# First feed-forward of a decoder block: seven block products for eight in four units of its last product, with a weight ring of five

## The chip, the cores and the metric

The kernel runs on one core of a Trainium2 chip. The time is the device time of one execution in microseconds (us), the median of several runs; shorter is better. The program is one launch, and all data start and end in the chip's main memory (HBM).

The engines are named as in the profile: PE is the matrix engine (PEld its weight loads), DVE the vector engine, ACT the scalar engine, POOL the general one, SP the engine that issues nearly all DMAs here. A matmul leaves its result in a PSUM bank of 128 x 512 float32, of which there are eight.

## The reference

One layer on 256 tokens of 1024 features, all in float32: a feed-forward, a token-mixing part, a second feed-forward, a last norm. What matters here is the first line:

```python
def swiglu(x, w_gate, w_up, w_down):
    return (jax.nn.silu(x @ w_gate) * (x @ w_up)) @ w_down

h = h + 0.5 * swiglu(rmsnorm(h, ffn1_norm), ffn1_w_gate, ffn1_w_up, ffn1_w_down)
n = rmsnorm(h, mix_norm)
z = n @ w_in                      # queries, keys, values and the gated branch, from n
# attention and spatial gating, sigmoid gates, one output projection, added to h
h = h + 0.5 * swiglu(rmsnorm(h, ffn2_norm), ffn2_w_gate, ffn2_w_up, ffn2_w_down)
return rmsnorm(h, final_norm)
```

The hidden width is 2816, so that `w_down` is 2816 x 1024: 22 blocks of 128 rows.

## The kernel before

**Three matmuls for a product.** Every float32 operand is split into a high part (a cast to the matrix engine's rounded float32, on ACT, L239) and a low part (value minus high part, on DVE, L241). A block product, 128 tokens x 128 features times 128 x 512 weights, is then three matmuls (`mm3`, L232 to L236): high by high, high by low, low by high.

**Weights come in units.** A unit is 1 MB in HBM, as a rule four 128 x 512 blocks, fetched as two halves of 512 KB into a ring of seven raw tiles (`RAW`, L161) and split into one tile of a ring of four (`RING`, pool `wp`). `unit(i, ahead)` (L200) sees to it that the splits of all units up to i + ahead stand in the programs of ACT and DVE before the matmuls of unit i; with `ALONE` that is three units ahead. A split of unit i + 3 or later overwrites a ring tile and so waits until PE has read its last occupant. Each split of a half also puts the fetch of the half seven places on into SP's queue, which waits until that raw tile is free.

**Order of work.** PE and SP do what they are told in the order of the program text. DVE and ACT are ordered by a scheduler in the two feed-forwards' first products, and by the text inside `with in_order():`, which holds the whole of the first feed-forward's last product and what follows it up to the second feed-forward. Each engine runs its own list strictly in order, and an instruction that waits holds up all behind it.

**First feed-forward.** Its first product runs in eleven chunks of 256 hidden features, two units each (`chunk`, L447; tiles `f`). Behind a chunk, `glu` (L486) makes the hidden values by tokens, and they go through HBM to be turned: `leave` writes a chunk (`f1way`), `arrive` reads four blocks of 128 hidden features back (`f1back`, one buffer), `settle` splits them (`f1h`). The last product (L658 to L677, tiles `down`) has 11 units f1d of four blocks each. It goes through the 1024 output features in two halves of 512: first half f = 0, all 22 hidden blocks for both token blocks j, then f = 1. At the end of a half, `add` (L640) adds the bank to the residual by tokens (`ht1`), transposes it in 32 x 32 squares, writes it to HBM (`h_way`) and squares it; `from_way` reads it back by features into `h`. `norm_parts(f)` (L653) makes high and low parts of the normed half (`nT2`) out of `h`. `norm_parts(0)` stands behind the ninth unit's matmuls. Then come q, k and gv: the products over the first half of the features for all three (`chunk(..., [0])`), `norm_parts(1)` among them, then those over the second half.

**Seven products for eight.** The second feed-forward's last product (`down`, L355) already treats the units in `SEVEN` = 0, 2, 4, 6 otherwise. A unit is there two hidden blocks by two feature halves, and with two token blocks a 2 x 2 by 2 x 2 block product of eight 128 x 128 x 512 products. Winograd's form of Strassen's scheme needs seven. It takes sums of the weight quarters (`quarters`, L175: four adds on DVE) and of the hidden blocks (`form`, L512: four DVE operations and a split). Such a unit fills two ring tiles: "single" (three quarters as they are) and "sums" (four sums); only the first is fetched. Products go to four banks of their own (`shared` 1, 5, 6, 7) and to the ordinary ones (`acc`). `settle_seven` (L402) folds the shared banks into the output with a copy on ACT, four adds and four multiply-adds on DVE.

## Time and profile before

| | us |
|---|---|
| median of 3 runs (lowest, highest) | 522.43 (522.08, 522.85) |
| the profiled execution's own time | 522.75 |
| its span, first to last instruction | 520.6 |
| PE busy in the span | 512.6 |
| DVE busy | 378.7 |
| ACT busy | 273.3 |
| mean of DMA traffic | 244 GB/s |

An execution's time is some 2 us longer than its span: 522.75 beside 520.6 here. The mean granted clock of the matrix engine is 0.998 of full speed. Durations in the rows are those of single instructions; neighbours on one engine overlap somewhat, so that the distance between two starts can be shorter than a duration. That is so above all for matmuls: one has a duration of 0.39 us and the next starts 0.23 us after it.

For orientation, the profile has the first product of the first feed-forward up to 125.6 us, its last product from there to 185.5 us, q, k and gv to 218 us, and the second feed-forward's last product from 456.9 to 511.7 us.

### The profile page before, as it was taken

To read this page: it belongs to the slowest core of one execution; us is meant where nothing else is said; L and a number is where in the kernel's file an instruction comes from. 1 tells how busy PE (TensorE), PEld (TensorE's weight loads), DVE (VectorE), ACT (ScalarE), POOL (GpSimd) and SP (SyncE) were. 2 spreads that over 40 slices of the span, in tenths; PEclk is the share of its full clock that TensorE was granted. 3 is DMA by queue.
4 is the path that set the end of the run, shared out by engine and by line. 5 is a ranking of instruction groups with operands and counts; after the bars stand their busy time and mean duration, and the time that the engine had idled before them with its cause. 6 is when DMAs were issued, how large, how long until landed. Compare 5 with 4: busy or idle time off the path is not lost.

```text
span 520.6 us, 6736 instructions
## 1 busy us (share of the span) xinstructions
PE 512.6 (98%) x2389; PEld 426.9 (82%) x2389; DVE 378.7 (73%) x533; ACT 273.3 (52%) x382; POOL 12.0 (2%) x25
## 2 busy tenths in 40 slices
PE   9999999999999999999999999999999999999995
PEld 7888888888888888888888898888888888888884
DVE  6895757576455565669977687987866776799974
ACT  7755355464444545666656423666535544566712
POOL 0010000000000010000000000001000000000002
PEclk9999999999999999999999999999999999999999
DMA  8998598969876867597799756839689869459602
GB/s 314 369 346 300 154 360 259 259 211 293 240 248 199 285 192 255 153 304 270 187 346 326 264 172 170 313 95 339 210 220 314 274 262 326 148 178 280 225 0 81
DMA packets 63920, 126.80 MB, mean 244 GB/s; under 512 B 11664, under 2 KB 36752, under 8 KB 63760
## 3 DMA queue, kind: packets, MB, share of 16 engines
q1 hardware_dynamic: 63600, 126.06, 75.3%
q8 instruction: 18, 0.29, 0.2%
q10 hardware_dynamic: 288, 0.33, 0.2%
q14 instruction: 14, 0.11, 0.1%
HBM read 113.26 MB, written 13.11 MB: 243 GB/s over the span
## 4 chain that ended last, share of the span: by engine, by line
PE 93%; DMA 3%; DVE 1%; ACT 1%; SPq 1%; issue 1%; POOLq 0%; DVEq 0%; POOL 0%; ACTq 0%
PE f L234 15%; PE f L236 15%; PE f L235 15%; PE down L236 4%; PE down L234 4%; PE down L235 4%; PE acch L235 4%; PE acch L236 3%; PE acch L234 3%; PE acc L208 3%; PE g L234 3%; PE g L236 3%; PE g L235 3%; PE acc L213 1%; DMA raw<-in_gate 1%; PE f L586 1%
## 5 line engine op out<-in xcount | busy, mean ns | idle before, releaser
L241 DVE TENSOR_TENSOR w<-raw,w 128x1024 fp32r<-128x1024 f32 (+1 forms) x180 | 209.5, 1205 | 62.7 <-ACT w L239 62.7
L239 ACT CAST w<-raw 128x1024 fp32r<-128x1024 f32 (+1 forms) x180 | 177.6, 1038 | 84.0 <-PE f L236 46.6
L234 PE MATMUL f<-w,n 128*128 128x512 f32 x336 | 130.9, 389 | 0.0
L236 PE MATMUL f<-w,n 128*128 128x512 f32 x336 | 130.9, 389 | 0.0
L235 PE MATMUL f<-w,n 128*128 128x512 f32 x336 | 130.8, 389 | 0.0
L236 PEld LDWEIGHTS f<-w,n 128*128 128x128 f32 x336 | 63.1, 188 | 13.1
L235 PEld LDWEIGHTS f<-w,n 128*128 128x128 f32 x336 | 63.1, 188 | 13.1
L234 PEld LDWEIGHTS f<-w,n 128*128 128x128 f32 x336 | 63.1, 188 | 12.9
L235 PE MATMUL down<-w,f1h 128*128 128x512 f32 x88 | 34.3, 390 | 0.0
L234 PE MATMUL down<-w,f1h 128*128 128x512 f32 x88 | 34.3, 389 | 0.0
L236 PE MATMUL down<-w,f1h 128*128 128x512 f32 x88 | 34.3, 389 | 0.0
L236 PE MATMUL acch<-w,f2h 128*128 128x512 f32 x64 | 24.9, 390 | 0.0
L235 PE MATMUL acch<-w,f2h 128*128 128x512 f32 x64 | 24.9, 390 | 0.0
L234 PE MATMUL acch<-w,f2h 128*128 128x512 f32 x64 | 24.9, 390 | 0.0
L234 PE MATMUL g<-w,n 128*128 128x512 f32 x64 | 24.9, 390 | 0.0
L235 PE MATMUL g<-w,n 128*128 128x512 f32 x64 | 24.9, 389 | 0.0
L236 PE MATMUL g<-w,n 128*128 128x512 f32 x64 | 24.9, 389 | 0.0
L490 ACT ACTIVATE f2s<-f,rstd 128x256 f32<-128x256 f32 x22 | 10.3, 473 | 24.5 <-PE f L236 24.3
L490 ACT ACTIVATE f1s<-f,rstd 128x256 f32<-128x256 f32 x22 | 10.3, 473 | 24.3 <-PE f L236 22.8
L492 DVE SCALAR_TENSOR_TENSOR f2a<-f,rstd,f2s 128x256 f32<-128x256 f32 x22 | 10.1, 472 | 14.7 <-ACT f2s L490 14.4
L235 PEld LDWEIGHTS down<-w,f1h 128*128 128x128 f32 x88 | 16.5, 188 | 3.4
L234 PEld LDWEIGHTS down<-w,f1h 128*128 128x128 f32 x88 | 16.5, 188 | 3.4
(207 smaller groups left out, 711.5 us busy)
## 6 DMA issues: line engine op xcount, KB each, us to landing
raw<-in_f SPq DMA_DIRECT2D x84, 512.0 KB, 6.2
raw<-in_f1d SPq DMA_DIRECT2D x22, 512.0 KB, 5.5
raw<-in_f2d SPq DMA_DIRECT2D x22, 512.0 KB, 6.4
raw<-in_gate SPq DMA_DIRECT2D x16, 512.0 KB, 6.3
raw<-in_out SPq DMA_DIRECT2D x8, 512.0 KB, 5.8
f1way<-f1t SPq DMA_DIRECT2D x11, 256.0 KB, 6.6
f2way<-f2t SPq DMA_DIRECT2D x11, 256.0 KB, 5.1
front<-in_first SPq DMA_DIRECT2D x7, 384.0 KB, 6.0
```

What stands on the lines that cost most here:

```text
L208: nc.tensor.matmul(ps, st, both.rearrange("p two n -> p (two n)"), start=first, stop=last)
L213: nc.tensor.matmul(ps[:, n:], st, both[:, 0, :], start=False, stop=False)
L234: nc.tensor.matmul(ps, sh, mh, start=first, stop=False)
L235: nc.tensor.matmul(ps, sh, ml, start=False, stop=False)
L236: nc.tensor.matmul(ps, sl, mh, start=False, stop=last)
L239: nc.scalar.copy(hi, src)
L241: nc.vector.tensor_sub(lo, src, hi.bitcast(F32))
L490: nc.scalar.activation(sg, ps[j][:, :CH], AF.Silu, scale=rs[j])
L492: nc.vector.scalar_tensor_tensor(a, ps[j][:, CH:], rs[j], sg, op0=ALU.mult, op1=ALU.mult)
L586: nc.tensor.matmul(sums[0][j][:, c], st[j][0], hi[:, c], start=k + c.start == 0, stop=False)
```

## The change

The first feed-forward's last product uses the seven-product form too, in the units of hidden blocks 0 and 1, 4 and 5, 8 and 9, 12 and 13. These four units (f1s, laid out as in the second feed-forward) have both feature halves in them. The other 14 hidden blocks (`REST`) stay in seven plain units (f1d) that go through the feature halves one after the other as before. The order is seven-unit, plain unit, four times, then three more plain units: eleven in all. The bytes fetched are the same.

- `settle_seven` is in two parts: first the adds into features 0 to 511, and, as a function that is called later, those into features 512 to 1023. The second feed-forward calls both at once. In the first, the first part stands behind the fourth seven-unit's matmuls, and the second behind the end of half f = 0, in the middle of the fourth plain unit. For that unit and the fourth seven-unit the look-ahead is 1, so that no later unit's split stands between those steps on DVE and ACT. `norm_parts(0)` stands behind the fifth plain unit, with two plain units left.
- `form_behind` makes the hidden blocks' sums during the first product, in both feed-forwards.
- `RING` is 5. `ALONE` and `PAIRED` keep their values of 3 and 2; the new `DEEP` is 4 and is used in both feed-forwards' products (from the fourth chunk of the first one, from the third of the second) and in both last products.
- The four sums of a "sums" unit are all made ahead of its two splits; before, two of them stood ahead of each split. They take the raw tiles out of use earlier.
- To make room, `h` and the two tiles of forms share memory one after the other, the zeros of the warm-up use the memory of a later tile, the banks' sums use the pool of the weights' sums, and the memory set aside for descriptors of DMAs that software issues is set to 1024 bytes.

```diff
-RING = 4
+RING = 5
 RAW = 7
-ALONE = RING - 1
-PAIRED = RING - 2
+DEEP = RING - 1
+ALONE = RING - 2
+PAIRED = RING - 3
 SEVEN = (0, 2, 4, 6)
+REST = [k for k in range(FB) if k // 2 not in SEVEN]
+PLAIN = len(REST) // 2
...
-    zeros = small.tile([P, S], BF16, tag="zeros", name="zeros", bufs=1)
+    zeros = act.tile([P, S], BF16, tag="ws", name="zeros")
...
-    f1d = add_units("f1d", FB // 2)
+    f1d = []
+    for n in range(PLAIN):
+        if n < len(SEVEN):
+            f1d.append((len(units), n))
+            units.extend([("f1s", n, "single"), ("f1s", n, "sums")])
+        f1d.append((len(units), None))
+        units.append(("f1d", n))
...
-            (a, b), (c, d) = ([raws[i - 1, k][:, 0, n:n + 512] for n in (0, 512)] for k in range(2))
-            r, to = sump.tile([P, 2, 512], F32, tag="sum", name=f"sum{i}_{hf}"), w[:, 2 * hf:2 * hf + 2]
             if hf == 0:
-                raws[i] = r
-                nc.vector.tensor_add(r[:, 0], a, b)
-                nc.vector.tensor_add(r[:, 1], b, d)
-            else:
-                nc.vector.tensor_add(r[:, 0], raws.pop(i)[:, 0], d)
-                nc.vector.tensor_add(r[:, 1], r[:, 0], c)
+                (a, b), (c, d) = ([r[:, 0, n:n + 512] for n in (0, 512)] for r in [raws.pop((i - 1, k)) for k in range(2)])
                 for k in range(2):
-                    del raws[i - 1, k]
+                    raws[i, k] = sump.tile([P, 2, 512], F32, tag="sum", name=f"sum{i}_{k}")
+                first, second = raws[i, 0], raws[i, 1]
+                nc.vector.tensor_add(first[:, 0], a, b)
+                nc.vector.tensor_add(first[:, 1], b, d)
+                nc.vector.tensor_add(second[:, 0], first[:, 0], d)
+                nc.vector.tensor_add(second[:, 1], second[:, 0], c)
+            r, to = raws.pop((i, hf)), w[:, 2 * hf:2 * hf + 2]
         return split(to[:, :, 0, :], to[:, :, 1, :], r)
...
+    def product(banks, name, key, st, w, last):
+        first = key not in banks
+        if first:
+            banks[key] = bank(f"acc{name}" + "_".join(map(str, key)))
+        mm3(banks[key], st, w, first, last)
+    def seven(name, at, i, tokens_of, acc, shared, ahead=DEEP):
+        a, b, d = tokens_of(2 * i, 0), tokens_of(2 * i + 1, 0), tokens_of(2 * i + 1, 1)
+        last = i == SEVEN[-1]
+        def of(w, n):
+            return w[:, n, 0, :], w[:, n, 1, :]
+        def form(n):
+            return tuple(hidden.forms[i][:, n, two, :] for two in range(2))
+        w = unit(at, ahead)
+        product(shared, name, (1,), a, of(w, 0), last)
+        product(acc, name, (0, 0), b, of(w, 1), False)
+        product(acc, name, (0, 512), form(3), of(w, 2), False)
+        w = unit(at + 1, ahead)
+        product(shared, name, (5,), form(0), of(w, 0), last)
+        product(shared, name, (7,), form(1), of(w, 1), last)
+        product(shared, name, (6,), form(2), of(w, 2), last)
+        product(acc, name, (1, 0), d, of(w, 3), False)
+    def settle_seven(name, shared, scale, hh):
+        p1, p5, p6, p7 = (shared[n,] for n in (1, 5, 6, 7))
+        both = sump.tile([P, 2, 512], F32, tag="sum", name=f"both{name}")
+        m, u = both[:, 0], both[:, 1]
+        def add(x, by, j, c0):
+            to = hh[:, j, c0:c0 + 512]
+            nc.vector.scalar_tensor_tensor(to, x, by, to, op0=ALU.mult, op1=ALU.add)
+        nc.scalar.copy(u, p1)
+        add(p1, scale, 0, 0)
+        nc.vector.tensor_add(u, p6, u)
+        nc.vector.tensor_add(m, p7, u)
+        add(m, scale, 1, 0)
+        def rest():
+            nc.vector.tensor_add(u, p5, u)
+            add(u, -scale, 0, 512)
+            nc.vector.tensor_add(m, p5, m)
+            add(m, -scale, 1, 512)
+        return rest
...
-        def seven(i):
...
-        def settle_seven():
-            p1, p5, p6, p7 = (shared[n,] for n in (1, 5, 6, 7))
-            m = tmp.tile([P, 512], F32, tag="hg", name=f"m{name}")
-            nc.scalar.copy(m, p1)
-            add(p1, 0, 0, 512)
-            nc.vector.tensor_add(m, p6, m)
-            u = tmp.tile([P, 512], F32, tag="hg", name=f"u{name}")
-            nc.vector.tensor_add(u, p5, m)
-            nc.vector.scalar_tensor_tensor(hh[:, 0, 512:], u, -scale, hh[:, 0, 512:], op0=ALU.mult, op1=ALU.add)
-            nc.vector.tensor_add(m, p7, m)
-            nc.vector.scalar_tensor_tensor(hh[:, 1, :512], m, scale, hh[:, 1, :512], op0=ALU.mult, op1=ALU.add)
-            nc.vector.tensor_add(m, p5, m)
-            nc.vector.scalar_tensor_tensor(hh[:, 1, 512:], m, -scale, hh[:, 1, 512:], op0=ALU.mult, op1=ALU.add)
...
-                    settle_seven()
+                    settle_seven(name, shared, scale, hh)()
             else:
-                w = unit(at[i], ALONE)
+                w = unit(at[i], DEEP)
...
-    def chunk(i0, nT, name, c, us=range(2), ps=None, apart=1):
-            w = unit(i0 + 2 * c + apart * u, ALONE)
+            w = unit(i0 + 2 * c + apart * u, ahead)
...
+        def form_behind(self, c, tags):
+            p, odd = divmod(c - 4, 2)
+            for i in SEVEN if p >= 0 and not odd else ():
+                if i // 2 == p:
+                    n = SEVEN.index(i)
+                    if n % 2 == 0:
+                        self.two = act.tile([P, 2, 4, 2, P], F32R, tag=tags[n // 2], name=f"{self.name}forms{n}")
+                    self.form(p, i % 2, self.two[:, n % 2])
...
-            sums.append(chunk(f1, nT, "f1", c))
+            sums.append(chunk(f1, nT, "f1", c, ahead=DEEP))
+            hidden.form_behind(c, ("h", "nC"))
             for moved in (1, 2, 3) if c == 3 else (c,):
...
+    h = act.tile([P, 2, S // 32, P], F32, tag="h", name="h")
...
-        last = 2 * FB - 4
-        sums = [None, None]
-        for i in range(FB // 2):
-            w = unit(f1d + i, ALONE)
-            at = range(4 * i, 4 * i + 4)
-            for s, j in [(s, j) for j in range(NT) for s in at] if 4 * i == last else [(s, j) for s in at for j in range(NT)]:
-                f, b = divmod(s, FB)
-                if b == 0:
-                    sums[j] = bank(f"down1{f}{j}")
-                st = tuple(p[:, j * P:(j + 1) * P] for p in (hidden.aT[:, b, 0, :], hidden.aT[:, b, 1, :]))
-                mm3(sums[j], st, tuple(w[:, s % 4, two, :] for two in range(2)), b == 0, b == FB - 1)
-                if b == FB - 1:
-                    add(f, j, sums[j])
-                    if j == NT - 1:
-                        from_way(h[:, f], h_way[f])
-            for then in rest[i:i + 1]:
+        acc, shared, settled = {}, {}, []
+        def tokens_of(b, j):
+            return tuple(p[:, j * P:(j + 1) * P] for p in (hidden.aT[:, b, 0, :], hidden.aT[:, b, 1, :]))
+        for n, (at, s) in enumerate(f1d):
+            ahead = 1 if len(SEVEN) * 2 - 2 <= n < len(SEVEN) * 2 else DEEP
+            if s is not None:
+                seven("down1", at, SEVEN[s], tokens_of, acc, shared, ahead)
+                if s == len(SEVEN) - 1:
+                    settled.append(settle_seven("down1", shared, 0.5, ht1))
+            else:
+                w = unit(at, ahead)
+                slots = range(4 * units[at][1], 4 * units[at][1] + 4)
+                ends = slots[-1] == 2 * len(REST) - 1
+                for slot, j in [(x, j) for j in range(NT) for x in slots] if ends else [(x, j) for x in slots for j in range(NT)]:
+                    f, b = divmod(slot, len(REST))
+                    last = b == len(REST) - 1
+                    product(acc, "down1", (j, f * 512), tokens_of(REST[b], j),
+                            tuple(w[:, slot % 4, two, :] for two in range(2)), last)
+                    if last:
+                        add(f, j, acc[j, f * 512])
+                        if j == NT - 1:
+                            from_way(h[:, f], h_way[f])
+                            if f == 0:
+                                settled.pop()()
+            for then in rest[n:n + 1]:
                 then()
-            if i == FB // 2 - 3:
+            if n == len(f1d) - 3:
                 norm_parts(0)
...
-        ps = chunk(f2, nT3, "f2", c)
+        ps = chunk(f2, nT3, "f2", c, ahead=DEEP)
         if c == 2:
             hidden.move(1)
-        if c in (4, 6, 8, 10):
-            p = (c - 4) // 2
-            if p % 2 == 0:
-                forms = act.tile([P, 2, 4, 2, P], F32R, tag="h" if p == 0 else "nB", name=f"forms{p}")
-            hidden.form(p, 0, forms[:, p % 2])
+        hidden.form_behind(c, ("h", "nB"))
...
-    down1 = a["ffn1_w_down"][0][hidden][:, turned].reshape(FB, P, 2, 512).transpose(2, 0, 1, 3)
+    down1 = a["ffn1_w_down"][0][hidden][:, turned]
...
-        "f1d": down1.reshape(FB // 2, 4, P, 512).transpose(0, 2, 1, 3),
+        "f1s": rows(down1)[list(SEVEN)],
+        "f1d": down1.reshape(FB, P, 2, 512)[REST].transpose(2, 0, 1, 3).reshape(PLAIN, 4, P, 512).transpose(0, 2, 1, 3),
...
-    nc = bacc.Bacc("TRN2", target_bir_lowering=False, num_devices=1)
+    nc = bacc.Bacc("TRN2", target_bir_lowering=False, num_devices=1, dynamic_dma_scratch_size=1024)
```

More of the change, by code (lines that the diff above doesn't have):

```diff
@@ L61, in bank @@
         return psum.tile([P, 512], F32, tag="ps", name=name)
-    h = act.tile([P, 2, S // 32, P], F32, tag="h", name="h")
     def by_32(x):
@@ L369, in tokens_of @@
             return tuple(p[:, j * P:(j + 1) * P] for p in part_of(k))
-        def product(banks, key, st, w, last):
-            first = key not in banks
-            if first:
-                banks[key] = bank(f"acc{name}" + "_".join(map(str, key)))
-            mm3(banks[key], st, w, first, last)
         def ends(j, c0, k):
             return k == (K - 1 if (c0, 512) in cuts[j] else near - 1)
-        def seven(i):
-            a, b, d = tokens_of(2 * i, 0), tokens_of(2 * i + 1, 0), tokens_of(2 * i + 1, 1)
-            last = i == SEVEN[-1]
-            def of(w, n):
-                return w[:, n, 0, :], w[:, n, 1, :]
-            def form(n):
-                return tuple(hidden.forms[i][:, n, two, :] for two in range(2))
-            w = unit(at[i], ALONE)
-            product(shared, (1,), a, of(w, 0), last)
-            product(acc, (0, 0), b, of(w, 1), False)
-            product(acc, (0, 512), form(3), of(w, 2), False)
-            w = unit(at[i] + 1, ALONE)
-            product(shared, (5,), form(0), of(w, 0), last)
-            product(shared, (7,), form(1), of(w, 1), last)
-            product(shared, (6,), form(2), of(w, 2), last)
-            product(acc, (1, 0), d, of(w, 3), False)
@@ L445, in down, with chunk @@
                 done(hh, j, hf)
-    def chunk(i0, nT, name, c, us=range(2), ps=None, apart=1):
+    def chunk(i0, nT, name, c, us=range(2), ps=None, apart=1, ahead=ALONE):
         if ps is None:
```

5 lines of the change are left out of this document (2 added, 3 removed).

## The prediction

> **What bounds the kernel now.** I read the page first: busy times, the slices and the shares of the chain.
>
> ```profile
> span 520.6 us, 6736 instructions
> PE 512.6 (98%) x2389; PEld 426.9 (82%) x2389; DVE 378.7 (73%) x533; ACT 273.3 (52%) x382; POOL 12.0 (2%) x25
> PE   9999999999999999999999999999999999999995
> PE 93%; DMA 3%; DVE 1%; ACT 1%; SPq 1%; issue 1%; POOLq 0%; DVEq 0%; POOL 0%; ACTq 0%
> ```
>
> PE is busy in every slice but the last, and it makes 93% of the chain that ended last. So a matmul that goes away is time, if nothing else makes PE wait. DVE, at 73%, is the engine that could. Next the windows by stage (columns: window, its length, busy time and instructions of PE, PEld, DVE, ACT and POOL, granted clock, DMA share, GB/s): two stretches of the first product, the last product of the first feed-forward, and two stretches of the second feed-forward's last product, which has the seven-product form already.
>
> ```profile
> 81.90:103.70 21.80, 21.80 (x98) 18.07 (x97) 13.82 (x17) 10.66 (x14) 0.00 (x0) 1.00 0.86 250
> 103.70:125.50 21.80, 21.80 (x98) 18.07 (x97) 13.77 (x17) 10.65 (x14) 0.00 (x0) 1.00 0.85 232
> 125.62:185.46 59.84, 59.84 (x265) 49.57 (x264) 35.87 (x39) 28.37 (x36) 1.69 (x5) 1.00 0.78 246
> 467.00:477.00 10.00, 10.00 (x45) 8.28 (x45) 10.00 (x12) 5.76 (x7) 0.00 (x0) 1.00 0.73 191
> 477.00:487.00 10.00, 10.00 (x46) 8.26 (x44) 10.00 (x13) 6.97 (x9) 0.00 (x0) 1.00 0.96 357
> ```
>
> The stage to be changed has 264 matmuls (the 265th is the tail of the one before) in 59.84 us: 0.2267 us each, a block product 0.68 us. DVE is free there for 24 us, and for 8 us in each stretch before. Where the seven-product form already stands, DVE has no free time at all, and yet PE waited there once only:
>
> ```profile
> PEld acch L235 <- DVE w L241: 0.4, 1, 0.4
> ```
>
> **What goes.** Four units with one product fewer, three matmuls each: 12 x 0.2267 = **2.72 us**, all on the path. Bytes fetched stay, so DMA has to move the same in 57.1 us instead of 59.8; its share rises from 0.78 to about 0.82, below the 0.86 of a stretch in which PE never waited. I put it at nothing.
>
> **What DVE gets in addition.** The groups by line and shape give its prices (and ACT's cast).
>
> ```profile
> L241 DVE TENSOR_TENSOR w<-raw,w 128x1024 fp32r<-128x1024 f32 x176 | 207.0, 1217 | 62.7 <-ACT w L239 62.7
> L239 ACT CAST w<-raw 128x1024 fp32r<-128x1024 f32 x176 | 175.7, 1048 | 81.9 <-PE f L236 44.5 <-PE down L236 20.2 <-issue 7.1
> L241 DVE TENSOR_TENSOR w<-sum,w 128x1024 fp32r<-128x1024 f32 x8 | 9.8, 1221 | 1.1 <-ACT w L239 1.1
> L241 DVE TENSOR_TENSOR w<-raw,w 128x512 fp32r<-128x512 f32 x4 | 2.7, 667 | 0.0
> L186 DVE TENSOR_TENSOR sum<-raw 128x512 f32<-128x512 f32 x4 | 2.7, 684 | 0.0
> L241 DVE TENSOR_TENSOR forms<-f2form,forms 128x512 fp32r<-128x512 f32 x4 | 2.7, 686 | 1.4 <-ACT forms L239 1.4
> L519 DVE TENSOR_TENSOR f2form<-f2back 128x128 f32<-128x128 f32 x4 | 1.1, 286 | 1.6 <-DMA f2back<-f2way 1.6
> L492 DVE SCALAR_TENSOR_TENSOR f1a<-f,rstd,f1s 128x256 f32<-128x256 f32 x22 | 10.2, 469 | 10.5 <-ACT f1s L490 10.4
> L493 DVE STREAM_TRANSPOSE f1t<-f1a 128x256 f32<-128x256 f32 x22 | 9.0, 431 | 0.3
> L241 DVE TENSOR_TENSOR f1h<-f1back,f1h 128x1024 fp32r<-128x1024 f32 x5 | 6.1, 1220 | 5.5 <-ACT f1h L239 5.5
> ```
>
> A "single" unit costs DVE 0.667 + 1.217 = 1.88 us, a "sums" unit 4 x 0.684 + 2 x 1.221 = 5.18, a plain one 2 x 1.217 = 2.43, the forms of a unit 4 x 0.286 + 0.686 = 1.83, `glu` 2 x (0.469 + 0.431) = 1.80. A seven-unit with the plain unit behind it takes DVE 9.5 us, and PE 15 x 0.68 = 10.2 us.
>
> With a ring of five and four units ahead, the split of the first seven-unit may begin when PE starts the second-last chunk. From there to DVE's arrival at the fold it does four "single" (7.5), four "sums" (20.7), five plain units (12.2), three `glu` (5.4), two forms (3.7) and the settling of the last hidden blocks (3 x 1.22 + 0.68 = 4.3): 53.8 us. PE takes from there to the sixth product of the fourth seven-unit, the last bank that the fold's first part needs, 4 x 5.44 + 3 x 4.76 + 3 x 5.44 + 4.08 = 56.4 us. So DVE gets there 2.6 us early if its durations add up and it never waits. They add up to less, as the sums of the second feed-forward show on DVE's timeline:
>
> ```profile
> 461.06 0.69 DVE L186 TENSOR_TENSOR sum<-raw 128x512 f32<-128x512 f32 x1
> 461.66 0.68 DVE L187 TENSOR_TENSOR sum<-raw,raw 128x512 f32<-128x512 f32 x1
> 462.26 0.69 DVE L189 TENSOR_TENSOR sum<-sum,raw 128x512 f32<-128x512 f32 x1
> ```
>
> Starts lie 0.60 apart under a duration of 0.69. Taken for all of DVE's work, 0.60 for 0.69 makes it 47 us and the lead 9 us; I keep 2.6 to 9, which leaves some us for waits. The Trainium skill, "VectorE: DVE Perf Modes", section "The DRAIN you can't avoid", says that the next operation cannot start until the pipeline has emptied, so that durations would add up; these rows overlap and disagree. By that rule the lead is the 2.6 us, and PE still does not wait.
>
> **The fold and what it holds up.** On DVE, before, at the end of the first half (w30 is the ninth unit of f1d, w31 the tenth):
>
> ```order
> L241 TENSOR_TENSOR w30_1358<-raw30_0_1229,w30_1358 128x2x512
> L241 TENSOR_TENSOR w30_1358<-raw30_1_1260,w30_1358 128x2x512
> L642 SCALAR_TENSOR_TENSOR ht1_470<-down100_1184,ht1_470 128x512
> L644 STREAM_TRANSPOSE turnedh00_1377<-ht1_470 128x512
> L642 SCALAR_TENSOR_TENSOR ht1_470<-down101_1188,ht1_470 128x512
> L644 STREAM_TRANSPOSE turnedh01_1389<-ht1_470 128x512
> L241 TENSOR_TENSOR w31_1415<-raw31_0_1264,w31_1415 128x2x512
> ```
>
> And now (w34, just ahead, is the fifth plain unit, and the next row is the split of w35, the sixth; accdown11, 16, 17 and 15 are the shared banks, accdown10_0 and accdown11_0 the ordinary ones of the first half):
>
> ```order
> L397 SCALAR_TENSOR_TENSOR ht1_469<-accdown11_1223,ht1_469 128x512
> L401 TENSOR_TENSOR bothdown1_1482<-accdown16_1252,bothdown1_1482 128x512
> L402 TENSOR_TENSOR bothdown1_1482<-accdown17_1248,bothdown1_1482 128x512
> L397 SCALAR_TENSOR_TENSOR ht1_469<-bothdown1_1482,ht1_469 128x512
> L669 SCALAR_TENSOR_TENSOR ht1_469<-accdown10_0_1227,ht1_469 128x512
> L671 STREAM_TRANSPOSE turnedh00_1498<-ht1_469 128x512
> L669 SCALAR_TENSOR_TENSOR ht1_469<-accdown11_0_1256,ht1_469 128x512
> L671 STREAM_TRANSPOSE turnedh01_1510<-ht1_469 128x512
> L406 TENSOR_TENSOR bothdown1_1482<-accdown15_1244,bothdown1_1482 128x512
> L397 SCALAR_TENSOR_TENSOR ht1_469<-bothdown1_1482,ht1_469 128x512
> L408 TENSOR_TENSOR bothdown1_1482<-accdown15_1244,bothdown1_1482 128x512
> L397 SCALAR_TENSOR_TENSOR ht1_469<-bothdown1_1482,ht1_469 128x512
> ```
>
> Eight rows more stand between splits, and all that follows on DVE waits for PE's end of the first half. The same work in the trace, and the way of the second half out to HBM and back (DVE, SP, ACT, DVE, and PE's first use of it):
>
> ```profile
> 156.39 0.69 DVE L642 SCALAR_TENSOR_TENSOR ht<-down,ht 128x512 f32<-128x512 f32 x1
> 158.43 0.71 DVE L644 STREAM_TRANSPOSE turnedh<-ht 128x512 f32<-128x512 f32 x1
> 185.46 0.39 PE L234 MATMUL q<-w,n 128*128 128x512 f32 x1
> 186.39 0.71 DVE L644 STREAM_TRANSPOSE turnedh<-ht 128x512 f32<-128x512 f32 x1
> 190.18 1.96 SPq L465 DMA_DIRECT2D h<-hway x4
> 196.38 1.71 ACT L301 ACTIVATE n<-h,cols 128x256 fp32r<-128x256 f32 x4 [3.29 <-DMA h<-hway]
> 196.93 1.69 DVE L305 SCALAR_TENSOR_TENSOR n<-h,cols,n 128x256 fp32r<-128x256 f32 x4 [2.38 <-ACT n L301]
> 201.78 0.39 PE L234 MATMUL q<-w,n 128*128 128x512 f32 x1
> raw<-in_k SPq DMA_DIRECT2D x4, 512.0 KB, 6.1
> raw<-in_bg SPq DMA_DIRECT2D x4, 512.0 KB, 8.5
> ```
>
> Let T be the moment at which PE ends the third seven-unit. The first half's last products for the two token blocks end at T + 5.44 + 4.76 + 2.04 = T + 12.2 and T + 12.9. Add and transpose of both took 156.39 to 159.14, 2.75 us; the fold's second part is four operations of that length, about 2.75. DVE is through at T + 12.4 + 5.5 = T + 17.9, and the two subs of w35 (2.4) are done at T + 20.3. PE wants w35 at T + 21.1: **0.8 us to spare**, the tightest place of the stage. I take no wait; the bounds are 0 and, with DVE late at the fold, what it is late beyond 2.6 + 0.8.
>
> **The halves' return.** `norm_parts` stands in order on ACT and DVE behind w38's split. From the end of the second transpose to the first high part took 187.10 to 196.38, 9.3 us, and SP had issued the read back 5.0 us after that end. Now the first half's transposes end at T + 15.2; the read is issued by T + 20.2, and only behind it, in SP's queue, comes the fetch of the second half of w38 (k's). At 6.1 us it lands at T + 26.3; cast 1.05, four high parts 1.71: T + 29.1. PE wants the first block at T + 32.0. The two splits that follow (w39, w40) end at about T + 29.1 + 4 x 1.05 + 1.2 = T + 34.4, and only then does DVE's list come to the second half's adds, which PE has ready at T + 32.0:
>
> ```order
> L247 TENSOR_TENSOR w39_1607<-raw39_0_1547,w39_1607 128x2x512
> L247 TENSOR_TENSOR w39_1607<-raw39_1_1551,w39_1607 128x2x512
> L247 TENSOR_TENSOR w40_1640<-raw40_0_1556,w40_1640 128x2x512
> L247 TENSOR_TENSOR w40_1640<-raw40_1_1560,w40_1640 128x2x512
> L669 SCALAR_TENSOR_TENSOR ht1_469<-accdown10_512_1231,ht1_469 128x512
> L671 STREAM_TRANSPOSE turnedh10_1662<-ht1_469 128x512
> ```
>
> These rows stood in the same order before, but there the first half had come back long before, and DVE waited for PE. Second transpose: T + 37.2, 5.2 us behind the start of q, where it was 187.10 - 185.46 = 1.6. So the second half comes 3.6 us later against PE. It had 201.78 - 197.4 = 4.4 us to spare: **0.8 us left**. Bounds: 4.4 left if DVE is waiting again; with the 8.5 us of the slowest weight fetches for 6.1, 1.6 short.
>
> **At nothing:** ACT's casts and copies, since half of its time is free, and the eight PSUM banks. The last bank that the first seven-unit takes, for its seventh product, is the last chunk's. `glu` reads that one from 125.65 on, the instant the chunk ends, while PE wants it six products or 4.1 us later:
>
> ```profile
> 125.65 0.48 DVE L492 SCALAR_TENSOR_TENSOR f1a<-f,rstd,f1s 128x256 f32<-128x256 f32 x1 [1.83 <-ACT f1s L490]
> ```
>
> Without that cover it would cost DVE's lateness there. The deeper ring can at most save the one wait of 0.4 in the second feed-forward. That the seventh product is gone is certain: PE's list has 2342 rows for 2354.
>
> **Sum.** The profiled execution took 522.75 with a span of 520.6; less 2.72 that is 520.0 and 517.9. It lies 0.32 above the median of the runs, so the median goes to 522.43 - 2.72 = **519.7**.
>
> **Rivals.** *A, the second half returns late* (chance 0.2): PE waits between gv and the second half of q, by 0.3 to 1.6 us: about 520.7. For it: the margin of 0.8 above; against it: a weight fetch behind little else lands sooner, as v's do (below). *B, the same with the fold late too* (0.1): 1.7 to 3.7 us, the gain is eaten: 521.4 to 523.4, within 0.2% of before (which is what a measurement can tell apart). *C, slower* (0.07): DVE falls behind in the seven-units, as it did in the second feed-forward, and reaches the fold late; everything behind the fold waits in order. It decides from 2.6 + 0.8 = 3.4 us of waits on, and costs the excess. In the profile ACT waits once for the returning hidden blocks, and DVE for ACT (5.5 in the row of f1h above): alone that is a price of 2.1. With one more wait for a ring tile, 3.1, it is 5.2: 519.7 + 5.2 = 524.9. Against it: PE lives with a fully busy DVE at 467 to 487, with a ring of four. The rows: v's fetches, DVE's wait for a ring tile in the last product, and the warm-up's matmuls.
>
> ```profile
> raw<-in_v SPq DMA_DIRECT2D x4, 512.0 KB, 4.8
> 154.11 2.36 DVE L241 TENSOR_TENSOR w<-raw,w 128x1024 fp32r<-128x1024 f32 x2 [3.09 <-ACT w L239]
> 1.18 3.81 PE L101 MATMUL warm<-zeros 128*128 128x256 bf16 x17 [1.18 <-DVE zeros L98]
> ```
>
> At the start a matmul of 256 columns takes 0.224 us, as long as one of 512 later: half speed. The Trainium skill, "TensorE: Matmul & The Clock Gate", section "What's actually happening", has the clock drop to half after an idle window of about 3.4 us, until as long a busy one; no pause in this trace is long enough to show it. By that rule C's pause would cost 1.7 us more, an estimate from the page, and give 526.6.
>
> **Chances.** No new wait (519.3 to 520.1): 0.6; A 0.2, B 0.1, C 0.07; 0.03 for still faster. Faster by over 0.2% (under 521.4): 0.83; within: 0.10; slower: 0.07. The range of 519.2 to 521.4 leaves out B and C.
>
> **What would show it.** PE has 2377 matmuls, and the stage lasts 57.1 us. PE's waits list nothing on tiles w or n between the last chunk and q's second half; if they do, `seven` or w35 names C, n behind h the rivals A and B. DVE should be busy for some 60 of the 68 us from the second-last chunk to the sixth plain unit. Wrong would be a span above 519.

## The result and the profile after

The change takes **519.33 us** (median of 6 runs, 518.86 to 520.45) where the kernel before, run beside it, takes 522.64 (522.08 to 522.91): a ratio of 0.994 with a 95% interval of 0.9927 to 0.9953, so faster by 2.5 to 3.8 us. Predicted were 519.7 and a range of 519.2 to 521.4. The profiled execution took 519.43 with a span of 517.7 (predicted 517.9).

The page of the change: span, busy times, PE's slices and the shares of the chain.

```profile
span 517.7 us, 6795 instructions
PE 509.5 (98%) x2377; PEld 424.0 (82%) x2377; DVE 403.9 (78%) x585; ACT 281.1 (54%) x395; POOL 12.0 (2%) x25
PE   8999999999999999999999999999999999999995
PE 94%; DMA 2%; DVE 1%; issue 1%; SPq 1%; ACT 0%; POOLq 0%; DVEq 0%; POOL 0%; ACTq 0%
```

PE is still busy in every slice. It has 12 matmuls fewer and 3.1 us less busy time; DVE has 25 us more. The windows by stage (columns as in the prediction): first the changed stage, then the stretch from the second-last chunk to the sixth plain unit.

```profile
126.27:183.39 57.12, 57.12 (x253) 47.30 (x252) 51.88 (x63) 35.31 (x44) 0.51 (x3) 1.00 0.69 226
104.58:172.51 67.93, 67.93 (x301) 56.24 (x300) 58.74 (x80) 38.21 (x49) 1.48 (x3) 1.00 0.65 205
```

The stage took 59.84 us and takes 57.12: 2.72 less, to the hundredth what twelve matmuls take, and PE is busy in all of it. DVE went from 35.87 us of work in 59.84 to 51.88 in 57.12. The view of waits lists two for PE in the whole span, both at the start:

```profile
PE warm L101 <- DVE zeros L98: 1.2, 1, 1.2
PE f L610 <- ACT n L586: 0.9, 1, 0.9
```

Now the fold and w35 on DVE, and PE's first two matmuls on w35 (timeline; "x5" joins neighbours of one kind, the first two of these five are w35's subs).

```profile
161.15 0.69 DVE L401 TENSOR_TENSOR bothdown<-accdown,bothdown 128x512 f32<-128x512 f32 x1 [1.39 <-PE accdown L242]
163.87 0.69 DVE L669 SCALAR_TENSOR_TENSOR ht<-accdown,ht 128x512 f32<-128x512 f32 x1 [0.58 <-PE accdown L242]
169.18 5.76 DVE L247 TENSOR_TENSOR w<-raw,w 128x1024 fp32r<-128x1024 f32 x5
172.51 0.39 PE L240 MATMUL accdown<-w,f1h 128*128 128x512 f32 x1
172.74 0.39 PE L241 MATMUL accdown<-w,f1h 128*128 128x512 f32 x1
```

DVE arrives at the fold at 159.08, makes its first add there and then waits 1.39 us for PE. T, the end of the third seven-unit, is 151.43 here. w35's two subs are done at 171.53, T + 20.1; PE begins w35 at T + 21.1. And the way of the second half, as in the prediction: SP's write and read, ACT's high parts, PE's first use.

```profile
185.85 1.65 SPq L672 DMA_DIRECT2D hway<-turnedh  x2
191.97 2.40 SPq L480 DMA_DIRECT2D h<-hway  x4
196.72 1.71 ACT L307 ACTIVATE n<-h,cols 128x256 fp32r<-128x256 f32 x4 [7.62 <-DMA h<-hway]
199.71 0.39 PE L240 MATMUL q<-w,n 128*128 128x512 f32 x1
```

Outside the changed stage the two profiled spans differ by little, with signs both ways: the first matmul of the first product comes 0.8 us later in the change (5.91 for 5.09 us; 5.09 again in the change's second profile), the waits of 0.6 at v (in the attention part) and of 0.2 in the second feed-forward's last product are absent.

### The profile page after: what moved, and what is told of

It reads as the page before. It is cut to its first block, busy times and chain, and to the rows that moved or that the text cites. A ratio compares the mean times of both kernels' runs of the same rounds, so it can differ in the third digit from the quotient of the medians.

```text
span 517.7 us, 6795 instructions
## 1 busy us (share of the span) xinstructions
PE 509.5 (98%) x2377; PEld 424.0 (82%) x2377; DVE 403.9 (78%) x585; ACT 281.1 (54%) x395; POOL 12.0 (2%) x25
## 4 chain that ended last, share of the span: by engine, by line
PE 94%; DMA 2%; DVE 1%; issue 1%; SPq 1%; ACT 0%; POOLq 0%; DVEq 0%; POOL 0%; ACTq 0%
PE f L242 15%; PE f L241 15%; PE f L240 15%; PE accdown L242 4%; PE accdown L241 4%; PE accdown L240 4%; PE acch L242 4%; PE acch L241 4%; PE acch L240 3%; PE acc L214 3%; PE g L241 3%; PE g L242 3%; PE g L240 3%; DMA raw<-in_gate 1%; PE acc L219 1%; DMA front<-in_first 1%
## 5 line engine op out<-in xcount | busy, mean ns | idle before, releaser
L247 DVE TENSOR_TENSOR w<-raw,w 128x1024 fp32r<-128x1024 f32 (+1 forms) x180 | 207.2, 1194 | 36.6 <-ACT w L245 36.1
L240 PE MATMUL f<-w,n 128*128 128x512 f32 x336 | 130.7, 389 | 0.0
L241 PE MATMUL f<-w,n 128*128 128x512 f32 x336 | 130.7, 389 | 0.0
L241 PEld LDWEIGHTS f<-w,n 128*128 128x128 f32 x336 | 63.1, 188 | 13.2
L240 PEld LDWEIGHTS f<-w,n 128*128 128x128 f32 x336 | 63.1, 188 | 13.1
L240 PE MATMUL accdown<-w,f1h 128*128 128x512 f32 x68 | 26.5, 389 | 0.0
L241 PE MATMUL accdown<-w,f1h 128*128 128x512 f32 x68 | 26.5, 389 | 0.0
L242 PE MATMUL accdown<-w,f1h 128*128 128x512 f32 x68 | 26.5, 389 | 0.0
L245 ACT CAST w<-sum 128x1024 fp32r<-128x1024 f32 x16 | 16.7, 1053 | 16.9 <-DVE sum L195 13.1
L240 PE MATMUL g<-w,n 128*128 128x512 f32 x64 | 24.9, 389 | 0.0
L241 PE MATMUL g<-w,n 128*128 128x512 f32 x64 | 24.9, 389 | 0.0
L240 PE MATMUL acch<-w,f2h 128*128 128x512 f32 x64 | 24.9, 389 | 0.0
L241 PE MATMUL acch<-w,f2h 128*128 128x512 f32 x64 | 24.9, 389 | 0.0
L247 DVE TENSOR_TENSOR w<-sum,w 128x1024 fp32r<-128x1024 f32 x16 | 19.3, 1216 | 1.2 <-ACT w L245 1.2
```

The costliest lines, as they stand in the source:

```text
L240: nc.tensor.matmul(ps, sh, mh, start=first, stop=False)
L241: nc.tensor.matmul(ps, sh, ml, start=False, stop=False)
L242: nc.tensor.matmul(ps, sl, mh, start=False, stop=last)
L245: nc.scalar.copy(hi, src)
L247: nc.vector.tensor_sub(lo, src, hi.bitcast(F32))
```

## The experiments

All kernels were timed beside the kernel before, which had medians of 522.52, 522.54 and 522.61 in the three sets. "The change" below is 519.2, its time in the first set.

### The change again

Nothing edited.

> The change itself once more, on the chip of the runs beside it. Theory (the twelve matmuls are the gain): ratio to the kernel before about 0.994, 519.2 to 519.8 us; the stage from the first unit of the last product to the start of q is 57.1 us again, with no wait of PE in it. If the wait of 0.65 us before v, which the profile of before has and that of the change has not, belongs to the change, it is missing again; if it is the hap of a DMA, it may stand in either.

Measured: 519.21 us (518.99 to 519.56), ratio 0.9931 (0.9918 to 0.9944). The stage takes 57.12 us again, without a wait. At v, PE waited 1.1 us this time:

```profile
PE v L240 <- DVE mixed L771: 1.1, 1, 1.1
```

So the v wait was missing from the first profile of the change by chance: with the order of v unchanged, the profiles of this study show 0 to 1.1 us of it, whatever else was edited. It is not shown to be a part of the gain.

### Ring and order without the seven products

The last product makes its eight products in all units again; the hidden blocks' sums, which only the seven products use, are not made. The edit is shown in part.

```diff
-    f1d = []
-    for n in range(PLAIN):
...
+    f1d = add_units("f1d", FB // 2)
...
-            if s is not None:
-                seven("down1", at, SEVEN[s], tokens_of, acc, shared, ahead)
...
+        for i in range(FB // 2):
+            w = unit(f1d + i, DEEP)
```

> All of the change but its main part: the first feed-forward's last product does its eight products in all eleven units again, with the ring of five, the deeper look-ahead and the sums ahead of the splits kept. Theory (the twelve matmuls are the gain, the ring is at most the 0.4 us wait of the second feed-forward): 0.3 us under the kernel before, 0.9 at most if the wait of 0.65 before v goes with the ring too; the stage takes 59.8 us. Rival (ring and look-ahead are a main part of the gain of 3.3): 1 us or more under it.

Measured: 521.94 us, ratio 0.9985 (0.9977 to 0.9994): 0.6 under before (0.3 to 1.2). The stage takes 59.84 us again. Between this kernel and the change lie 2.73 us; twelve matmuls are 2.72. That they agree so closely is luck, since each time is known to some 0.5 us, but the size fits and the theory stands. What else the change brings is some 0.6 us.

### The change with a ring of four

```diff
-RING = 5
+RING = 4
-ALONE = RING - 2
-PAIRED = RING - 3
+ALONE = RING - 1
+PAIRED = RING - 2
```

> The change with a ring of four in place of five (look-ahead of three units where it was four). Theory: the tightest place is the sixth plain unit, w35, behind the fold; in this order of DVE its split ends about 0.8 us later than PE wants it, and the wait of 0.1 to 0.4 in the second feed-forward's last product is back: 0.8 to 1.5 us over the change, 520.2 to 521 us, with PE waiting on w35. Rival (seven products need no deeper ring, the fold is not tight): within 0.3 of the change.

Measured: 519.54 us, ratio 0.9938 (0.9923 to 0.9953): not to be told from the change. The expectation of 0.8 to 1.5 more was wrong. w35's second sub ended at 172.75 and PE began w35 at 172.13, 0.62 us earlier, without waiting. The low part of the tile's first half was done at 171.62. So PE does not want the whole tile when it begins; the next runs measure what it wants.

### A slower fold: 4, 6, 8 and 12 adds more

Behind the fold's second part, n adds of 128x512 on DVE whose result nothing uses.

```diff
                                 settled.pop()()
+                                idle = sump.tile([P, 2, 512], F32, tag="sum", name="idle")
+                                for k in range(n):
+                                    nc.vector.tensor_add(idle[:, k % 2], ht1[:, 0, :512], ht1[:, 1, :512])
```

> The change with eight more adds of 128x512 on DVE behind the second part of the fold, whose result nothing uses: 4.8 (starts 0.60 apart) to 5.5 us (durations of 0.69). The margin at w35 was 0.98 us in the trace of the change. Theory (the fold holds up w35, and PE waits for it as a whole): 3.8 to 4.5 us over the change, about 523.5, and slower than before. If PE waits for each half of the ring tile by itself, the first half has 2.1 us to spare: 2.7 to 3.4. Rival (the fold is not tight, other work behind it moves ahead or has slack): below 1 us.

> The change with four more adds of 128x512 on DVE behind the second part of the fold, whose result nothing uses. In the run with eight they took 0.60 each, so these take 2.4 us. That run also showed that PE's first matmul on w35 (high part by high part) did not wait for DVE, and the second one did, for the low part of the tile's first half. The margin of the change at w35 is then not 0.98 but about 2.4 us: the first half's low part is done at 169.5 where PE wants it at 171.9. Theory as mended: no wait at w35, 0 to 0.1; the second half of the features comes back up to 2.4 us later against a margin of 1.4 to 2.2, so that PE may wait 0 to 1.0 on n in q's second half: change +0 to 0.6. Theory as predicted (the tile is wanted whole, 0.8 to 1.0 to spare): +1.4 to 1.8, with the wait at w35. Rival: +0, since the return is set by the DMAs ahead of it and not by DVE.

> The same with six more adds, 3.6 us. With eight, PE stood still for 2.5 us at w35 and then ran its next nine matmuls at 0.43 us in place of 0.227, another 1.7 us. Theory (margin 2.4, and the clock falls only after a pause longer than this one): PE waits 1.2 us at w35 on the low part, no slow matmuls behind it, change +1.2. If the shorter pause brings the clock down too: +2.5 to 3. Theory as predicted (margin 0.98 for the whole tile): a wait of 2.6.

> The change with twelve more adds behind the fold, 7.2 us, for PE's clock after a pause. Pauses of 1.5 and 2.5 us (between the starts of two matmuls) were followed by matmuls at 0.227 us, one of 2.76 us by nine at up to 0.43. Theory (w35 has 2.3 to spare; a longer pause costs the same stretch of slow matmuls): a pause of about 5.1, then again nine or so slow ones, 1.7 us; with 0 to 1 for the second half on top, change +6.5 to 7.5. If the slow stretch grows with the pause: more than 8. If only the pause counts: +4.9.

| adds | time us (interval of the ratio) | wait at w35 | slow matmuls behind it | wait at q's second half |
|---|---|---|---|---|
| 0 | 519.21 (0.9918 to 0.9944) | 0 | 0 | 0 |
| 4 | 519.47 (0.9933 to 0.9957) | 0.12 | 0.1 | 0 |
| 6 | 521.34 (0.9963 to 0.9984) | 1.33 | 0.1 | 1.4 |
| 8 | 523.20 (0.9996 to 1.0015) | 2.53 | 1.7 | 0 |
| 12 | 526.10 (1.0059 to 1.0083) | 4.93 | 1.7 | 0 |

The three right columns are from the profiles: the distance between the starts of two matmuls less the usual 0.227, and for the slow ones the sum of what they took over 0.227. The profiled execution with 6 adds was the longest of its runs (522.83). PE at w35 with 4 and with 8 adds:

```profile
171.97 0.39 PE L240 MATMUL accdown<-w,f1h 128*128 128x512 f32 x1
172.32 0.50 PE L241 MATMUL accdown<-w,f1h 128*128 128x512 f32 x1
```

```profile
171.69 0.39 PE L240 MATMUL accdown<-w,f1h 128*128 128x512 f32 x1
174.45 0.50 PE L241 MATMUL accdown<-w,f1h 128*128 128x512 f32 x1 [2.37 <-DVE w L247]
174.79 0.59 PE L242 MATMUL accdown<-w,f1h 128*128 128x512 f32 x1
175.17 0.63 PE L240 MATMUL accdown<-w,f1h 128*128 128x512 f32 x1
175.60 0.63 PE L241 MATMUL accdown<-w,f1h 128*128 128x512 f32 x1
```

The matmul that waits is the second on w35 (L241, high by low), never the first (L240, high by high, made by ACT long before). It wants the low part of the tile's first half. In the change that is done at 169.18 + 1.22 = 170.40 and wanted at 172.74: **2.34 us to spare**. The waits follow it: an add takes 0.60 us there, and 4, 6, 8 and 12 of them less 2.34 make 0.06, 1.26, 2.46 and 4.86, each within 0.1 of what was measured. With the ring of four it was 172.36 - 171.62 = 0.74 us to spare.

By its time alone, the run with 8 adds would have confirmed the wrong theory: 4.0 us over the change, where a tile wanted as a whole was to cost 3.8 to 4.5. That is luck. The wait was 2.53, as for a tile wanted part by part, and the rest is slow matmuls, which no theory of that run had. With 4 and 12 adds the mended expectations came out (0.3 and 6.9 over the change). With 6 adds the wait at w35 did, but the time is 2.1 over where 1.2 was expected: the profile has a wait at q's second half besides.

With 8 adds the nine matmuls behind the pause are slow, most of them 0.43 us apart where 0.227 is usual. That is the clock: these are the windows of those 3.35 us with 8 adds, and of the 3.5 us behind the pause with 12 (the third column from the end is the granted clock).

```profile
174.45:177.80 3.35, 3.35 (x9) 2.63 (x10) 3.35 (x4) 0.00 (x0) 0.00 (x0) 0.56 0.56 169
```

```profile
177.20:180.70 3.50, 3.46 (x8) 2.78 (x9) 3.50 (x4) 0.00 (x0) 0.00 (x0) 0.51 0.62 176
```

In these two profiled executions twice the pause brings the same slow stretch, 1.7 us. Behind pauses of 1.55 and 1.64 us (6 adds) and of 2.52 (the look-ahead, below), between two starts, the granted clock stayed at 1.00.

That does not make a least pause or a fixed price. The granted clock reads 0.50 from 174.83 to 178.22 with 8 adds, from 0.4 us behind the pause on, and from 177.21 to 180.60 with 12, from its last moment on: the fall follows neither the pause's start nor its end at a fixed distance. And executions of one kernel differ. The mean granted clock of an execution of the change is 0.996 to 0.999. With 8 adds it is 0.997 or 0.998 in the four fastest of eleven executions (522.04 to 522.87 us) and 0.994 to 0.996 in the other seven (523.09 to 523.80), so that in some of them the clock seems not to have fallen. With 12 adds it is 0.994 or 0.995 in four of six (525.5 to 526.2), and 0.992 in the other two (527.3), which seem to have paid more. What decides beside the length stays open.

### Both parts of the fold at once

```diff
-                    settled.append(settle_seven("down1", shared, 0.5, ht1))
+                    settle_seven("down1", shared, 0.5, ht1)()
...
-                            if f == 0:
-                                settled.pop()()
```

> The change with both parts of the fold at once, right behind the fourth unit of seven products, so that nothing of it stands between the first half's last products and the split of w35. If its operations (about 2.5 us) fit where DVE waits for PE there, w35 is ready 2.4 us earlier and the first half's transposes are as before. Theory: no place on PE's path changes, change +0 (within 0.3). Rival (the first half's adds are held up by 2 us, its read back comes later and the splits of w38 to w40 and the second half's adds with it): +0.3 to 1.0, with PE waiting on n.

Measured: 519.58 us (518.96 to 521.33), ratio 0.995 (0.9937 to 0.9963): 0.4 over the change, intervals overlapping. The rival's mechanism is in the profile, small:

```profile
199.86 0.50 PE L240 MATMUL q<-w,n 128*128 128x512 f32 x1 [0.59 <-ACT n L307]
```

The second half's write was issued at 188.25 here, T + 37.4, and at T + 34.4 in the change. Three us later use up what it has to spare. The premise of the theory failed too: DVE waits for PE there for 0.58 us in the change, too short for the 2.5 us of the fold's second part. The first half's transposes ended 2.0 us later, and the low part of w35's first half was done at T + 19.5, not earlier than in the change (T + 19.0) but 0.5 later.

### Look-ahead of four throughout

```diff
-            ahead = 1 if len(SEVEN) * 2 - 2 <= n < len(SEVEN) * 2 else DEEP
+            ahead = DEEP
```

> The change without the shorter look-ahead around the fold: the splits of w35 and w36 stand ahead of the fold on DVE and ACT, that of w37 ahead of the first half's adds. Theory: the first half's transposes come some 4.6 us later, its read back and normed blocks too, and the second half some 3 us later, against a margin of 1.4 to 2.2: change +0.8 to 1.6, PE waiting on n for one of the halves. Rival (the second half's return is set by the DMAs ahead of it, and DVE's order has the slack): within 0.3.

Measured: 522.11 us (519.88 to 524.26), ratio 0.9995 (0.9982 to 1.0008): nearly all of the gain is gone, 2.9 over the change and twice the 0.8 to 1.6 that was expected. The profile has the expected wait, 2.3 us long, and no other that is new. The eleven times are spread over 4.4 us, so the wait is hardly the same in all.

```profile
198.92 0.39 PE L242 MATMUL gv<-w,n 128*128 128x512 f32 x1
201.44 0.50 PE L240 MATMUL q<-w,n 128*128 128x512 f32 x1 [2.13 <-ACT n L307]
201.77 0.40 PE L241 MATMUL q<-w,n 128*128 128x512 f32 x1
```

PE's matmul follows the start of ACT's high parts by 0.56 us (200.88 to 201.44). By that the second half had 199.71 - 196.72 - 0.56 = 2.4 us to spare in the first profile of the change, and 198.87 - 196.71 - 0.56 = 1.6 in the second. Against T the first write was issued 2.4 us later than in the change with 4 adds, 3.0 with the fold at once, and 3.5 here, and PE waited 0, 0.8 and 2.3. It isn't one to one: from the first write's issue to the last read's landing passed 10.9 us in the change (185.85 to 196.70; 11.7 in its second profile) and 10.6, 11.0 and 12.0 in these three. Just ahead of these writes stand weight fetches of 512 KB, and a write took 4.7 to 6.6 us to land. In the change the first half's two writes took 2.0 and 2.1 us; the last fetch ahead of them landed 0.7 us behind the first one's issue. That the fetches make the difference is read from this order; no run moved them.

### The sums two and two

```diff
                 nc.vector.tensor_add(first[:, 0], a, b)
                 nc.vector.tensor_add(first[:, 1], b, d)
+                raws[i] = (first, second, c, d)
+            else:
+                first, second, c, d = raws.pop(i)
                 nc.vector.tensor_add(second[:, 0], first[:, 0], d)
                 nc.vector.tensor_add(second[:, 1], second[:, 0], c)
```

> The change with the four sums of a unit made two and two, ahead of each of its splits, as in the kernel before. DVE does the same work; the raw tiles come free some 1.2 us later. Theory: with the ring of five the seven-units have 3.5 us and more to spare, so change +0 (within 0.3), no wait of PE on w in either last product. Rival (the sums ahead of the splits, not the ring, took away the 0.21 us of waits in the second feed-forward): those waits are back, +0.2.

Measured: **523.67 us**, ratio 1.0023 (1.0014 to 1.0032): 4.5 us over the change, slower than before. Neither the theory nor the rival saw it. PE's waits (three of its rows):

```profile
PE accdown L244 <- DVE w L250: 1.8, 2, 1.1
PE q L243 <- ACT n L310: 0.8, 1, 0.8
PE accdown L243 <- ACT w L248: 0.4, 1, 0.4
```

DVE at the third seven-unit's "sums", in this kernel and, in the second fence, in the change (its run beside the first set):

```profile
142.22 0.69 DVE L194 TENSOR_TENSOR sum<-raw 128x512 f32<-128x512 f32 x1
142.82 0.68 DVE L195 TENSOR_TENSOR sum<-raw,raw 128x512 f32<-128x512 f32 x1
144.70 1.23 DVE L250 TENSOR_TENSOR w<-sum,w 128x1024 fp32r<-128x1024 f32 x1 [1.20 <-ACT w L248]
145.84 0.68 DVE L199 TENSOR_TENSOR sum<-sum,raw 128x512 f32<-128x512 f32 x1
146.56 0.69 DVE L200 TENSOR_TENSOR sum<-sum,raw 128x512 f32<-128x512 f32 x1
148.37 1.22 DVE L250 TENSOR_TENSOR w<-sum,w 128x1024 fp32r<-128x1024 f32 x1 [1.12 <-ACT w L248]
```

```profile
138.07 0.68 DVE L194 TENSOR_TENSOR sum<-raw 128x512 f32<-128x512 f32 x1
138.68 0.68 DVE L195 TENSOR_TENSOR sum<-raw,raw 128x512 f32<-128x512 f32 x1
139.28 0.68 DVE L196 TENSOR_TENSOR sum<-sum,raw 128x512 f32<-128x512 f32 x1
140.00 0.69 DVE L197 TENSOR_TENSOR sum<-sum,raw 128x512 f32<-128x512 f32 x1
140.61 2.43 DVE L247 TENSOR_TENSOR w<-sum,w 128x1024 fp32r<-128x1024 f32 x2
```

A sub waits for ACT's cast of the sums that DVE has just made. In pairs, DVE stands still for that twice per unit, 2.3 us. With all four ahead, the second pair covers the first cast, and the first sub the second. Measured from the stage's start, the split of the "sums" unit is done 2.5, 5.2 and 7.6 us later in the second, third and fourth seven-unit than in the first profile of the change, which had 6.5, 3.6 and 4.3 to spare there. (The first one's stands in the first product, where the scheduler orders DVE, and is not later.) From there PE waits: 0.2 at the third unit, 1.7 at the fourth, 1.3 at w35, 1.1 at q's second half and again 0.2 in the second feed-forward: 4.5 us, as much as the medians differ (the profiled execution itself, at 524.33, lies 0.7 above its kernel's median).

Why the kernel before could make them in pairs in its second feed-forward: there the scheduler orders DVE and puts other work between. At the unit whose rows the prediction quotes, all four sums stand in a row (L186, L187, L189, and L190 at 462.98). At the next two the third sum and a weight split stand ahead of the first sub, and the fourth sum with more splits ahead of the second. The first feed-forward's last product is ordered by the text.

### Sums ahead, but neither seven products nor the ring of five

The kernel of the second experiment (eight products throughout) with the ring of four.

```diff
-RING = 5
+RING = 4
```

> Eight products in all units of the first feed-forward's last product, the ring of four, and from the change only what is left: the four sums ahead of the splits, the forms in their own function, the memory. Theory (the waits of 0.21 us in the second feed-forward's last product go by the sums, as the change with a ring of four had none): kernel before -0.2 to -0.5, as with the ring of five. Rival (the ring did it): kernel before, within 0.2, the waits still there.

Measured: 522.05 us, ratio 0.9992 (0.9983 to 1.0), and the waits in the second feed-forward's last product are absent. They go by the sums ahead of the splits, not by the ring: the kernel with the sums two and two has the ring of five, and the waits are back in it. By time alone this kernel can be told neither from before nor from the one with the ring of five.

### The scores' adds ahead of a split

```diff
-        chunk(mu, nT2, "u", 0, [1], psu)
+        chunk(mu, nT2, "u", 0, [1], psu, ahead=2)
```

> The change with a look-ahead of two in place of three at u's second half, so that the split of w47 (2.3 us on DVE) stands behind the adds that empty the scores' banks, and not ahead of them. All profiles so far, of before too, have a wait of 0 to 1.1 us of PE at v for these adds (before 0.65, the change 0 and 1.1). Theory: the adds begin as soon as the scores are there, the wait is 0, w46 and w47 keep over 5 us to spare: change -0.5 (-1.0 to 0). Rival (the adds wait for the scores themselves, or PE then waits for w47): 0 to +0.5.

Measured: **518.71 us** (518.40 to 519.05), ratio 0.9925 (0.9913 to 0.9937), the fastest kernel of the study. DVE ahead of v in the change (its second profile) and here (L771 empties the banks that v needs):

```profile
226.81 4.62 DVE L247 TENSOR_TENSOR w<-raw,w 128x1024 fp32r<-128x1024 f32 x4
231.35 2.61 DVE L771 TENSOR_TENSOR mixed<-sc,mask 128x512 f32<-128x512 f32 x6
```

```profile
226.22 2.35 DVE L247 TENSOR_TENSOR w<-raw,w 128x1024 fp32r<-128x1024 f32 x2
228.49 2.60 DVE L771 TENSOR_TENSOR mixed<-sc,mask 128x512 f32<-128x512 f32 x6
```

The adds begin 2.9 us earlier (3.1 against the start of q), and PE has no wait at v in the profile. The 0.5 us fit the wait of 0 to 1.1; the intervals of the two ratios overlap, so by time alone the gain isn't secured.

## Why the prediction was right, and where it was not

**What goes: right.** 12 x 0.2267 = 2.72 was the stage's difference, in both profiles of the change, and the kernel that has all else of it keeps the 59.84. The bytes cost nothing, but the estimate of DMA's share of 0.82 was not met: it is 0.69, with 226 x 57.12 = 12.9 MB moved in the stage where it was 246 x 59.84 = 14.7, so that some fetches moved out of it.

**What else goes: 0.4 us under the forecast.** By the kernel before that was timed beside it the gain is 3.3 us, 0.6 over the 2.72. The sum had no term for it. The prediction gave the deeper ring at most the one wait of 0.4 in the second feed-forward. The wait cost 0.2 by the distances of the matmuls, and it went, but by the sums, not by the ring. The two kernels without the seven products lie 0.5 and 0.6 under before; what is beyond the 0.2 lies inside their intervals and stays open.

**DVE in addition: right that it suffices, and the lead within its bounds.** 58.7 us busy of 67.9 fit the "some 60 of the 68". The lead at the fold was to be 2.6 to 9 us, waits not counted. DVE arrived at 159.08 and had the last bank that it needs at 161.15, 2.1 us ahead (2.8 in the second profile), with 6.9 us (5.6) of waits for ACT behind it, 3.0 of them for the returning hidden blocks. Without those the lead is 8 to 9 us. Part of that is an earlier start than the prediction had: three of the first unit's sums were begun before PE's second-last chunk, the first at 102.64. The section of the Trainium skill that the prediction set against its rows ("VectorE: DVE Perf Modes", "The DRAIN you can't avoid") also says that an operation which is not held starts earlier. Starts 0.60 us apart under durations of 0.69 do not contradict that.

```profile
L247 DVE TENSOR_TENSOR f1h<-f1back,f1h 128x1024 fp32r<-128x1024 f32 (+1 forms) x4 | 4.3, 1082 | 3.0 <-ACT f1h L245 3.0
L507 DVE SCALAR_TENSOR_TENSOR f1a<-f,rstd,f1s 128x256 f32<-128x256 f32 x6 | 2.9, 476 | 2.7 <-ACT f1s L505 2.7
```

**The step that failed, though the time came out: the sums ahead of the splits had no term.** A "sums" unit was costed as 4 x 0.684 + 2 x 1.221 = 5.18 us of DVE, with no wait in it. That is true only because all four sums stand ahead; in pairs the unit takes 2.3 us more, three such units bring DVE 7.6 us behind, and the change loses to the kernel before. That is rival C (DVE late in the seven-units, from 3.4 us of waits on, 524.9), with 523.67 measured. The prediction didn't see that one edit of the change held it off. It could have been read: the row of w<-sum has 1.1 us of idle behind ACT's cast, and the rows of sums that it quotes have the third sum right behind the second, with no sub between, which the text of the kernel before does not say. The ring of five, which the prediction needed for its lead, was worth nothing that the time shows: with four it is 519.54, and w35 keeps 0.74 us for 2.34.

**The fold: the time right, the margin wrong.** w35's split came at T + 20.1 where T + 20.3 was forecast. But "PE wants w35 at T + 21.1" took the tile as one. The matmul that waits is the second, and for the first half's low part alone: 2.34 us to spare, not 0.8, in both profiles. It is no tighter than the halves' return, with 2.4 and 1.6.

**The halves' return: the place right, the size off.** Predicted was a second transpose 5.2 us behind the start of q, and 0.8 us left; SP had issued its write at 187.17, 3.8 behind, and 1.6 to 2.4 were left. Three sizes were off. The fetch of the second half of w38 was issued at T + 19.4 and landed at T + 24.6, 5.2 us for the 6.1 taken, where the prediction had T + 26.3: it set the start of all that follows, and the transpose came 1.5 us sooner. The 4.4 us of before count from the first low part at 197.4, but PE's first matmul wants the high part alone: by 0.56 us behind its start, 201.78 - 196.38 - 0.56 = 4.8. Against that, the way from the transpose to the first high part took 9.6 and 10.4 us for 9.3. Rival A names the place that gave way first in two of the experiments, with the mechanism it gave.

**At nothing: right** for ACT and the banks: no wait of PE on either in the changed stage, in both profiles of the change.

**The clock.** The prediction set the sentence of the Trainium skill ("TensorE: Matmul & The Clock Gate", section "What's actually happening") beside rival C: half speed after an idle window of about 3.4 us, until as long a busy one, 1.7 us more. The change's trace has no such pause. The run with 12 adds has one, of 5.16 us between two starts, and the price in its profile is 1.7 us. With 8 adds a pause of 2.76 us, shorter than the Trainium skill's window, brought the clock down as well; one of 2.52 in another kernel did not. The half speed that the prediction read at the start rests on the durations of two kinds of matmul; the granted clock of that stretch reads 1.00 in the profile.

## What to carry to other kernels

Where one engine makes a value, a second one casts it and the first comes back for the remainder, put the independent work of the first engine between; in a list that is kept in order by hand nobody else will, and here it was worth more than the twelve matmuls. For the time to spare at a wait, find the instruction that really waits: here it was the second matmul on a tile, which reads the low part of half of it, and the margin was 2.34 us, not 0.8. Before believing that a wait in one profile went by an edit, look at a second profile of the same kernel: the one at v was 0 and 1.1 us in two profiles of the same code.

## What was not expected of the hardware

PE's granted clock fell to 0.50 for 3.4 us after a pause of 2.76 us between two matmuls' starts and after one of 5.16, 1.7 us of time either way in the two profiles; after pauses of 1.55, 1.64 and 2.52 us it did not fall. A wait can so cost more than it lasts: from 6 to 8 adds, 1.2 us more of work on DVE, w35 alone cost PE 2.8 us more in the profiles. But the same kernel's executions differ in their mean clock (0.994 to 0.998 with 8 adds, 0.992 to 0.995 with 12), so neither the length that is enough nor the price is settled by these pauses.

And a write of 256 KB, issued behind weight fetches, took 4.7 to 6.8 us to land, so that the way through HBM and back is 10.6 to 12.5 us and moves by more than some of the time to spare.
